# Weight loads of the dense pairs one pair sooner, high key/query stores issued by ScalarE, in a two-layer hybrid decoder trunk

## The chip, the cores and the metric

The kernel runs on 1 core of one Trainium2 chip. The metric is the device time of one launch in microseconds (us). Engines are named as in the profile: PE is TensorE, DVE is VectorE, ACT is ScalarE, POOL is GpSimd, SP is SyncE. SP has no arithmetic here: it issues DMAs. A DMA-issuing instruction is listed with a q after its engine (SPq).

## The reference, cut to what matters

All data are float32: x is 1 x 1024 x 1024, there are two layers, and each layer does

```python
h = rmsnorm(x, norm1[l])
proj = h @ w_in[l]                      # q, k, v of both mixers, and the gates
o_a = dilated_mixture(...)              # 12 heads of 64 in 3 groups: (window, dilation) = (128,1), (512,4), (2048,16)
o_b = stick_breaking_attention(...)     # 4 heads of 64
gates = sigmoid(gate_pre + b_gate[l]); g_a, g_b = gates[..., :1024], gates[..., 1024:]
x = x + (g_a * (o_a @ w_br[l, :256]) + g_b * (o_b @ w_br[l, 256:])) @ w_o[l]
h2 = rmsnorm(x, norm2[l])
a, v = split(h2 @ w_up[l])              # each 2816 wide
x = x + (gelu(causal_depthwise_conv(a)) * v) @ w_down[l]
```

and a last rmsnorm follows. The change touches only how the part `h @ w_in[l]` for the dilated groups 1 and 2 and for the gates is fed.

## The kernel before

**Split products.** Every float32 matrix product is done as three reduced-precision ones. An operand is split in two: ACT writes the high part (a cast, line 129), DVE subtracts it from the operand and writes the low part (line 130); `split` is that pair of instructions. PE then adds high x high, high x low and low x high.

**The mixer's items.** In each layer the attention work is a list of items: 16 stick-breaking items (named B), 4 near items (N, dilation 1) and 16 far items (T, the dilated groups 1 and 2). A far item makes scores z (line 584), DVE adds the bias and finds the row's extreme (line 795), ACT takes the exponential (796), PE transposes (803 to 805), `split` makes p1h and p1l, and PE applies them to the values (line 813). `attend` lets PE go on with a quantum of dense work (`Dense.advance`) after each piece of an item.

**The dense work.** The projections for groups 1 and 2 and for the gates come as fourteen pairs a layer: v1, k/q 1 of heads 0 and 1, k/q 2 of the same, v2, then k/q 1 and k/q 2 of heads 2 and 3, and eight gate pairs. A pair is a 2 x 2 block of products: 256 columns of weights by the two halves of the tokens. One block (token half 1, first columns) is done early and plainly by `ahead`; the first half of its sum is kept in DRAM as q1. The rest of a pair is done by `pair_rest` with fewer products: sums of weight blocks (on POOL and DVE: lines 990, 991, 993 and 998) meet sums of blocks of h (made once a layer by `block_sums`, tiles S[1] to S[4]). `seven` is one such product: 12 matmuls of 128 x 512 (lines 887 to 889). A pair needs five of them, with weight pieces called w6, w5, w7, w3 and w4 in that order of use; `piece` takes a slot for the high and the low part (four slots of each) and splits.

**Buffers around the change.** The raw weights of a pair are one tile `in_a` of four 128 x 512 blocks (a11, a12, a21, a22), with two slots (tag "ql"). Before the change the result r2 is written over a12, and the stores of r2 read it from there, so the slot stays taken until those are done. The tile `u` holds two blocks: u2 = a11 - a21 (made into w7) and u1, the q1 read back.

**The order.** PE follows the program's order. On ACT, DVE, POOL and SP a scheduler arranges the instructions of the mixer by when it expects them to be ready. Each engine then runs its list strictly in order. `Dense.ready` calls the first steps of a pair (up to `READY` = 6) while the pair before is being computed: the load of `in_a` is the first of these steps, so it stands in the program after the start of the pair before.

**Stores of keys and queries.** `put` in `pair_kq` writes a block's high part (tile kq_h) and low part, and stores both to DRAM (tk) as 64 x 4 x 128 pieces: 4 stores for a key block, 6 for a query block, 20 for a k/q pair (4 of them in `ahead`), all from SP. Far items read them back as t_kq (line 755), and values as t_v (line 761).

**Semaphores of DMAs.** DMAs that SP and ACT issue share eight completion semaphores by turns, and the program lets a DMA wait until the DMA eight before it in that count is complete.

Of the kernel before, what the change touches and what calls it, by code (L numbers as in the profile page):

```python
# [6 lines left out]
F32 = mybir.dt.float32  # L7
# [8 lines left out]
P = 128  # L16
# [36 lines left out]
def trunk_kernel(ctx, tc, x, norm1, w_in, b_gate, w_br, w_o, norm2, w_up, conv_w, conv_b, w_down, norm_f, out, depth=None, probe=None):  # L53
# [141 lines left out]
    class Dense:  # L195
# [2 lines left out]


        def __init__(self):  # L200
            self.main, self.plain, self.seven, self.done = [], [], [], set()
            self.side, self.later, self.hooks = [], {}, []
            self.now = self.nxt = None
            self.due, self.count = 0.0, 0
            self.started = False
            self.scored = self.applied = self.kq = self.v = 0
# [686 lines left out]
    def block_sums():  # L893


        keep = {}

        def first(t, a, b, i):
            if i == 0:
                if "r" not in keep:  # L900
                    keep["r"] = quarter("h_sum")
                new_s(t)
            r, (ah, al), (bh, bl) = keep["r"][:, i, :], a()[i], b()[i]
            pool.tensor_tensor(r, f32(al), f32(bl), ALU.subtract)
            pool.tensor_tensor(r, r, f32(ah), ALU.add)
            pool.tensor_tensor(r, r, f32(bh), ALU.subtract)

        def further(t, a, i):
            if t == 4:

                S[4] = half(0, 0)
            elif i == 0:
                new_s(t)
            r, (ah, al) = keep["r"][:, i, :], a()[i]
            dve.tensor_tensor(r, f32(ah), r, ALU.subtract)
            dve.tensor_tensor(r, r, f32(al), ALU.add)

        def in_two(t, i):
            split(*S[t][i], keep["r"][:, i, :])

        b11, b12, b21, b22 = (lambda n=n, k=k: half(n, k) for k in range(2) for n in (1, 0))
        todo = []

        def series(after, t, f, lag, gap):

            at = {}
            for i in range(4):
                at.setdefault(i * gap, []).append(lambda i=i: f(i))
                at.setdefault(i * gap + lag, []).append(lambda i=i: in_two(t, i))
            for k in range(3 * gap + lag + 1):  # L930
                todo.append((after, lambda fs=at.get(k, ()): [g() for g in fs]))

        series({"B17"}, 3, lambda i: first(3, b22, b12, i), 4, 3)
        series({"N01s"}, 1, lambda i: first(1, b12, b11, i), 4, 3)
        series({"N11s"}, 2, lambda i: further(2, b22, i), 1, 1)
        series({"plain", "01", "v0"}, 4, lambda i: further(4, b21, i), 1, 1)
        return todo
# [10 lines left out]
    def pair(dense, l, offs, tiled, put):  # L948

        key = offs[0]  # L950

        def view(x, n=None):

            return x.rearrange("p (r j) -> p r j", r=4) if tiled else x

        def grid(o):
            return o.rearrange("p (j r) -> p r j", r=4) if tiled else o

        def ahead():

            w = weights(w_in[l][:, offs[0] : offs[0] + P], P)
            yield
            t, f = small("q1s"), small("rf")
            o = bank("ps", "r_ps")
            yield from product(o, [(w[k], h_part(1, k)) for k in range(4)])
            act.copy(view(t), grid(o))
            nc.sync.dma_start(kept_product(key), t)
            yield
            o = bank("ps", "r_ps")
            yield from product(o, [(w[k], h_part(1, k)) for k in range(4, KD)])  # L970
            dve.tensor_tensor(view(f), view(t), grid(o), ALU.add)
            put(0, 1, f, False)
            yield

        return ahead, lambda: pair_rest(dense, l, offs, put, view, grid, kept_product(key))

    def pair_rest(dense, l, offs, put, view, grid, kept):

        raw = sb.tile([P, 4, 512], F32, tag="ql", bufs=2, name="in_a")
        for c in range(2):  # L980
            nc.sync.dma_start(
                raw[:, 2 * c : 2 * c + 2, :].rearrange("p a (k n) -> p (a k) n", n=P),
                w_in[l][:, offs[c] : offs[c] + P].rearrange("(k p) n -> p k n", p=P),
            )
        a11, a12, a21, a22 = (raw[:, i, :] for i in range(4))
        yield
        u = sb.tile([P, T], F32, tag="wr", bufs=NRAW, name="u")
        u1, u2 = u[:, HF:T], u[:, 0:HF]
        nc.sync.dma_start(u1, kept)
        pool.tensor_tensor(u2, a11, a21, ALU.subtract)  # L990
        pool.tensor_tensor(a21, a21, a22, ALU.add)  # L991
        yield
        dve.tensor_tensor(a11, a21, a11, ALU.subtract)
        w5 = piece(a21)
        yield
        w6 = piece(a11)
        yield
        pool.tensor_tensor(a11, a12, a11, ALU.subtract)
        yield
        w3 = piece(a11)  # L1000
        yield
        u5 = small("u5")
        pa, pc = bank("ps", "i_a"), bank("ps", "i_c")
        yield from seven(pa, w6, S[2], True, True)
        r2 = a12
        dve.tensor_tensor(view(r2), view(u1), grid(pa), ALU.add)
        w7 = piece(u2)
        yield "turn"
        yield
        yield from seven(pc, w5, S[1], True, True)  # L1010
        dve.tensor_tensor(view(u5), view(u1), grid(pc), ALU.add)
        w4 = piece(a22)
        dense.last(0)
        yield "turn"
        yield
        yield from seven(pa, w7, S[3], False, True)
        dve.tensor_tensor(view(u5), view(u5), grid(pa), ALU.add)
        put(1, 0, u5, False)
        yield "turn"
        yield  # L1020
        yield from seven(pc, w3, half(0, 1), False, True)
        dve.tensor_tensor(view(r2), view(r2), grid(pc), ALU.add)
        put(0, 0, r2, False)
        dense.last(1)
        yield "turn"
        yield
        for word in seven(pa, w4, S[4], False, True):
            yield "turn"
            yield
        dve.tensor_tensor(view(u1), view(u1), grid(pa), ALU.add)  # L1030
        put(1, 1, u1, False)
        yield

    def pair_kq(dense, l, g, pr):
        off = 256 * g + P * pr

        def put(c, n, x, psum):
            hi = small("kq_h", F32R)
            lo = small("kq_l", F32R) if psum else x.bitcast(F32R)
            hv, lv, xv = (t if t is x and psum else t.rearrange("p (r j) -> p r j", r=4) for t in (hi, lo, x))  # L1040
            if c:
                act.mul(hv, xv, -SCALE)
                dve.scalar_tensor_tensor(lv, xv, -SCALE, f32(hv), ALU.mult, ALU.subtract)
            else:
                act.copy(hv, xv)
                dve.tensor_tensor(lv, xv, f32(hv), ALU.subtract)
            for s in range(2):
                rows = slice(64 * s, 64 * s + 64)
                for src, kind, up in ((hv, c, 0), (hv, 1, 64), (lv, 2, 0)) if c else ((hv, 0, 0), (lv, 0, 64)):
                    there = tk[pr][s, :, up : up + 64, 3 * (g - 1) + kind, n * P : (n + 1) * P]  # L1050
                    nc.sync.dma_start(there.rearrange("r p j -> p r j"), f32(src[rows]))
            if (c, n) == (1, 1):
                dense.done.add(f"{g}{pr}")

        return pair(dense, l, (OFF_KA + off, OFF_QA + off), True, put)
# [63 lines left out]
    def mixer(l, pending):  # L1119
# [13 lines left out]
        dense.plain = [a() for a, _ in [*kqs.values(), *vs.values(), *gates]]  # L1133
        dense.seven = [rest() for _, rest in gates]
        dense.side = [({"B02"}, zeros)] * (l == 0) + block_sums()

        def kq(name, pr, after, off, scale):
# [707 lines left out]
```

## Time and profile before

| what | value |
|---|---|
| median of 3 runs | 2802.39 us (2801.98 to 2808.36) |
| the profiled execution | 2802.19 us, its span 2800.4 us |
| mean granted TensorE clock | 0.985 |
| layer 0: dense pairs beside near and far items, then gate pairs | about 330 to 615 us |
| layer 1: the same | about 1715 to 2005 us |

The profiled execution's own time is 0.2 us below the median, and 1.8 us of it lie outside the span. A page of the profile lists busy time by engine, the costliest groups of instructions with the idle time before them and what ended it, and the DMA issues; the trace behind it answers for any window. In a timeline row the columns are the start, the duration, engine, line, operation, tiles and count, and in brackets the idle time of the engine just before with what ended it. In a row of waits stand who waited for whom, the total, the number of times and the longest.

### The profile page before, as it was taken

The page shows a single profiled execution, that of the slowest core. Times are in us where ns is not written, and L with a number is a line of the kernel's source. Part 1 is how long each engine was busy: PE and PEld are TensorE (multiplying, and loading weights), DVE is VectorE, ACT ScalarE, POOL GpSimd, SP SyncE. Part 2 cuts the span into 40 slices and gives each one's busy share as a digit, 9 for nine tenths or more (in the row PEclk, how much of TensorE's full clock was granted, in tenths as well). Part 3 has the DMA queues.
Part 4 walks back from the last instruction along what each step waited for, and adds up shares of the span by engine and source line. Part 5 has one row for each costly group of instructions (what it writes and reads, how often), then busy time and mean ns, then how long its engine had stood idle before and what let it go on. Part 6 is the DMA issues. An engine that isn't in the chain of part 4 may idle for free. (4 is left out here: it accounts for less than half of the span.)

```text
span 2800.4 us, 37074 instructions
## 1 busy us (share of the span) xinstructions
PE 2689.2 (96%) x13098; PEld 2244.5 (80%) x13098; DVE 2087.0 (75%) x3132; ACT 1327.8 (47%) x2458; POOL 692.2 (25%) x509
## 2 busy tenths in 40 slices
PE   8998989989999999999999899889899999999999
PEld 8877868778888888878888778677788888888888
DVE  5886856656688888897657877565667899888965
ACT  5665524346455455532345655333454555554225
POOL 1004121213224343421210041121131334433210
PEclk9999999999999999999999999999999999999999
DMA  5033378545324444588411234775643344446873
GB/s 152 23 87 102 114 212 245 197 158 190 104 91 157 154 141 158 195 327 315 163 35 46 82 101 134 222 229 177 225 129 90 113 166 153 145 154 233 323 262 121
DMA packets 394629, 449.91 MB, mean 161 GB/s; under 512 B 22748, under 2 KB 315980, under 8 KB 392908
## 3 DMA queue, kind: packets, MB, share of 16 engines
q1 hardware_dynamic: 394444, 447.55, 48.5%
q8 instruction: 103, 1.69, 0.3%
q14 instruction: 82, 0.67, 0.1%
HBM read 300.61 MB, written 146.87 MB: 160 GB/s over the span
## 5 line engine op out<-in xcount | busy, mean ns | idle before, releaser
L130 DVE TENSOR_TENSOR w_lo<-up_a,w_hi 128x512 fp32r<-128x512 f32 x240 | 236.7, 993 | 20.2 <-ACT w_hi L129 20.2
L129 ACT CAST w_hi<-up_a 128x512 fp32r<-128x512 f32 x240 | 149.4, 622 | 184.1 <-PE u_a L888 45.8
L1601 DVE TENSOR_TENSOR x<-x,d_ps 128x512 f32<-128x512 f32 (+1 forms) x228 | 151.9, 671 | 77.0 <-PE d_ps L1595 75.6
L1332 POOL TENSOR_TENSOR cv<-cv 128x512 f32<-128x512 f32 x88 | 131.8, 1509 | 249.3 <-DVE cv L1327 139.4
L129 ACT CAST w_hi<-w_raw 128x512 fp32r<-128x512 f32 x176 | 109.2, 621 | 147.8 <-PE o_ps L156 68.3
L130 DVE TENSOR_TENSOR w_lo<-w_raw,w_hi 128x512 fp32r<-128x512 f32 x176 | 127.5, 728 | 69.5 <-ACT w_hi L129 68.7
L130 DVE TENSOR_TENSOR g<-cv,g 128x512 fp32r<-128x512 f32 x154 | 152.2, 989 | 5.2 <-ACT g L129 2.8
L1593 PE MATMUL d_ps<-gd_in,w_hi 128*128 128x512 f32 (+1 forms) x340 | 130.3, 383 | 2.3 <-ACT w_hi L129 1.1
L129 ACT CAST w_hi<-in_a 128x512 fp32r<-128x512 f32 x112 | 69.2, 619 | 131.6 <-POOL in_a L991 43.5
L990 POOL TENSOR_TENSOR u<-in_a 128x512 f32<-128x512 f32 x28 | 38.4, 1373 | 374.4 <-DMA in_a<-in_w_in_dram 211.9
L1595 PE MATMUL d_ps<-gd_in,w_lo 128*128 128x512 f32 (+1 forms) x340 | 129.8, 382 | 0.0
L1594 PE MATMUL d_ps<-gd_in,w_hi 128*128 128x512 f32 (+1 forms) x340 | 129.7, 382 | 0.0
L887 PE MATMUL u_a<-hh,w_hi 128*128 128x512 f32 x320 | 124.7, 390 | 0.5 <-DVE u L1483 0.5
L889 PE MATMUL u_a<-hh,w_lo 128*128 128x512 f32 x320 | 124.5, 389 | 0.0
L889 PE MATMUL u_a<-t_hi,w_lo 128*128 128x512 f32 x320 | 124.5, 389 | 0.0
L888 PE MATMUL u_a<-t_lo,w_hi 128*128 128x512 f32 x320 | 124.5, 389 | 0.0
L888 PE MATMUL u_a<-hl,w_hi 128*128 128x512 f32 x320 | 124.5, 389 | 0.0
L887 PE MATMUL u_a<-t_hi,w_hi 128*128 128x512 f32 x320 | 124.5, 389 | 0.0
L1593 PE MATMUL d_ps<-gd_in,wd 128*128 128x512 f32 (+1 forms) x292 | 113.9, 390 | 0.0
L1595 PE MATMUL d_ps<-gd_in,wd 128*128 128x512 f32 (+1 forms) x292 | 112.8, 386 | 0.0
L1594 PE MATMUL d_ps<-gd_in,wd 128*128 128x512 f32 (+1 forms) x292 | 112.8, 386 | 0.0
L129 ACT CAST g<-cv 128x512 fp32r<-128x512 f32 x154 | 94.9, 616 | 36.9 <-POOL cv L1332 29.4
(392 smaller groups left out, 8734.3 us busy)
## 6 DMA issues: line engine op xcount, KB each, us to landing
gd<-g SPq DMA_DIRECT2D x154, 512.0 KB, 3.6
gd_in<-gd SPq DMA_DIRECT2D x154, 512.0 KB, 6.6
up_a<-in_w_up_dram SPq DMA_DIRECT2D x80, 512.0 KB, 5.8
in_a<-in_w_in_dram SPq DMA_DIRECT2D x56, 512.0 KB, 5.5
w_raw<-in_w_in_dram SPq DMA_DIRECT2D x104, 256.0 KB, 3.0
t_kq<-tk SPq DMA_DIRECT2D x32, 768.0 KB, 5.4
wd_raw<-in_w_down_dram SPq DMA_DIRECT2D x22, 1024.0 KB, 8.4
gin<-gs SPq DMA_DIRECT2D x32, 512.0 KB, 4.4
```

What stands on the lines that cost most here:

```text
L129: act.copy(hi, src)
L130: dve.tensor_tensor(lo, src, f32(hi), ALU.subtract)
L887: pe.matmul(o, w[0][:, c], rh, start=(first and i == 0), stop=False, skip_group_check=True)
L888: pe.matmul(o, w[0][:, c], rl, start=False, stop=False, skip_group_check=True)
L889: pe.matmul(o, w[1][:, c], rh, start=False, stop=(last and i == 3), skip_group_check=True)
L990: pool.tensor_tensor(u2, a11, a21, ALU.subtract)
L1332: return lambda: pool.tensor_tensor(dst, a, b, ALU.subtract)
L1593: pe.matmul(o[:, sub], wh[:, c], gh[:, sub], start=(i == 0 and k in (0, 4, 5)), stop=False, skip_group_check=True)
L1594: pe.matmul(o[:, sub], wh[:, c], gl[:, sub], start=False, stop=False, skip_group_check=True)
L1595: pe.matmul(o[:, sub], wl[:, c], gh[:, sub], start=False, stop=(i == m - 1), skip_group_check=True)
L1601: dve.tensor_tensor(x, x, o[:, sub], ALU.add)
```

## The change

1. `pair_rest` gives back two things: the generator `run` and a function `load` that takes the `in_a` slot and issues the load. The loads of a layer are queued in `dense.loads` in the order of the pairs. When a pair has split its last piece w4, the next load in the queue is issued: that of the pair after the next. The first two pairs of a layer call their load at their own start, as all did before.
2. r2 is written into u2 instead of a12, so an `in_a` slot comes free when w4 is split.
3. The pieces are split in their order of use: w6, w5, w7 before the first product, w3 after it, w4 after the second. The two sums on POOL at the start are separate steps.
4. In `pair_kq`, stores whose source is the high part (12 of 20 a pair) are issued by ACT. Those of the low part stay on SP.
5. In `block_sums` the lag from a sum to its split goes from 4 steps to 6, and the gap from sum to sum from 3 to 4, for S[3] and S[1].

```diff
@@ block_sums
-        series({"B17"}, 3, lambda i: first(3, b22, b12, i), 4, 3)
-        series({"N01s"}, 1, lambda i: first(1, b12, b11, i), 4, 3)
+        series({"B17"}, 3, lambda i: first(3, b22, b12, i), 6, 4)
+        series({"N01s"}, 1, lambda i: first(1, b12, b11, i), 6, 4)
@@ pair_rest: the load becomes a function
+        raw = []
+        def load():
+            raw.append(sb.tile([P, 4, 512], F32, tag="ql", bufs=2, name="in_a"))
+            for c in range(2):
+                nc.sync.dma_start(
...
+        def run():
+            if not raw:
+                assert dense.loads.pop(0) is load
+                load()
...
-        dve.tensor_tensor(a11, a21, a11, ALU.subtract)
-        w5 = piece(a21)
-        yield
-        w6 = piece(a11)
-        yield
-        pool.tensor_tensor(a11, a12, a11, ALU.subtract)
-        yield
-        w3 = piece(a11)
-        yield
+            dve.tensor_tensor(a11, a21, a11, ALU.subtract)
+            w6 = piece(a11)
+            yield
+            pool.tensor_tensor(a11, a12, a11, ALU.subtract)
+            w5 = piece(a21)
+            yield
+            w7 = piece(u2)
+            yield
...
-        r2 = a12
+            r2 = u2
             dve.tensor_tensor(view(r2), view(u1), grid(pa), ALU.add)
-        w7 = piece(u2)
+            w3 = piece(a11)
...
             w4 = piece(a22)
+            if dense.loads:
+                dense.loads.pop(0)()
             dense.last(0)
@@ pair_kq, put
-                    nc.sync.dma_start(there.rearrange("r p j -> p r j"), f32(src[rows]))
+                    (nc.sync if src is lv else act).dma_start(there.rearrange("r p j -> p r j"), f32(src[rows]))
@@ mixer
+        order = [vs[1], *(kqs[g, 0] for g in (1, 2)), vs[2], *(kqs[g, 1] for g in (1, 2)), *gates]
+        dense.loads = [load for _, _, load in order]
```

What moves, in the lists of instructions of the engines. PE's list stays as it was, row for row. The list of SP in layer 0, before, around the load of the fourth pair, v2 (in_a_3839); tk0 and tk1 hold the stored keys and queries, tv the values, the numbers count buffers, and kq_h_3779 to u_3557 are blocks of the second pair:

```order
L1051 DMA tk0_90<-kq_h_3779 64x4x128 x2
L1051 DMA tk0_90<-u5_3705 64x4x128
L1051 DMA tk0_90<-kq_h_3805 64x4x128
L1051 DMA tk0_90<-in_a_3526 64x4x128
L1051 DMA tk0_90<-kq_h_3805 64x4x128
L1051 DMA tk0_90<-in_a_3526 64x4x128
L1051 DMA tk0_90<-kq_h_3830 64x4x128 x2
L1051 DMA tk0_90<-u_3557 64x4x128
L1051 DMA tk0_90<-kq_h_3830 64x4x128 x2
L1051 DMA tk0_90<-u_3557 64x4x128
L981 DMA in_a_3839<-in_w_in_dram 128x8x128 x2
L989 DMA u_3862<-q1_726 128x512
```

The same place on SP after the change (in_a_3760 is the fourth pair's load, in_a_3882 the fifth's; u_3740 belongs to the third pair, u_3862 to the fourth):

```order
L996 DMA u_3740<-q1_718 128x512
L1082 DMA tv1_93<-vv_3719 128x2x128 x2
L1082 DMA tv1_93<-vv_3724 128x2x128 x2
L983 DMA in_a_3760<-in_w_in_dram 128x8x128 x2
L1062 DMA tk0_90<-u5_3705 64x4x128 x2
L1062 DMA tk0_90<-u_3557 64x4x128 x4
L996 DMA u_3862<-q1_716 128x512
L983 DMA in_a_3882<-in_w_in_dram 128x8x128 x2
```

Before, a pair's load stands directly ahead of its own u and behind the second pair's stores; now the fourth pair's load stands ahead of those stores, and the fifth's directly behind the fourth pair's u: each a pair sooner. Of the sixteen stores that `pair_rest` makes for a k/q pair, six are left on SP.

ACT's list in layer 0 before, at the first far items (p1 rows are exponentials, p1h rows the high parts that PE waits for):

```order
L1042 ACTIVATE kq_h_4174<-u5_4091 128x512
L129 COPY w_hi_4214<-in_a_4088 128x512
L1045 COPY kq_h_4200<-in_a_3961 128x512
L796 ACTIVATE p1_4222,st1_4218<-p1_4222,st1_4218 128x256
L796 ACTIVATE p1_4222,st1_4218<-p1_4222,st1_4218 128x512
L129 COPY w_hi_4307<-u_4135 128x512
L1042 ACTIVATE kq_h_4244<-u_3984 128x512
L129 COPY p1h_4274<-t1_4270 128x384
L796 ACTIVATE p1_4255,st1_4218<-p1_4255,st1_4218 128x256
L796 ACTIVATE p1_4255,st1_4218<-p1_4255,st1_4218 128x512
```

The same place on ACT after:

```order
L1053 ACTIVATE kq_h_4172<-u5_4091 128x512
L1062 DMA tk1_91<-kq_h_4172 64x4x128 x4
L1056 COPY kq_h_4199<-u_3984 128x512
L129 COPY w_hi_4217<-u_4135 128x512
L1062 DMA tk1_91<-kq_h_4199 64x4x128 x2
L796 ACTIVATE p1_4225,st1_4221<-p1_4225,st1_4221 128x256
L796 ACTIVATE p1_4225,st1_4221<-p1_4225,st1_4221 128x512
L1053 ACTIVATE kq_h_4247<-u_3984 128x512
L129 COPY p1h_4277<-t1_4273 128x384
L1062 DMA tk1_91<-kq_h_4247 64x4x128 x2
L129 COPY p1h_4296<-t1_4292 128x384
L1062 DMA tk1_91<-kq_h_4247 64x4x128 x2
```

Ten DMA issues (six, two and two) now stand between ACT's own work and the exponentials and p1h casts behind them. Over both layers ACT's list gains 96 DMA issues, and SP's loses as many.

At the sums of h the wider spacing moves nothing: POOL's list there is the same before and after, and so are the places of the splits t_hi on ACT, in both layers. Before and after, the first of S[1]'s sums follow those of S[3] on POOL as

```order
L905 TENSOR_TENSOR h_sum<-h_sum,hh_108 128x512 x2
L906 TENSOR_TENSOR h_sum<-h_sum,hh_108 128x512 x2
L904 TENSOR_TENSOR h_sum<-hl_109,hl_363 128x512
L905 TENSOR_TENSOR h_sum<-h_sum,hh_108 128x512
L904 TENSOR_TENSOR h_sum<-hl_109,hl_363 128x512
L906 TENSOR_TENSOR h_sum<-h_sum,hh_362 128x512
L905 TENSOR_TENSOR h_sum<-h_sum,hh_108 128x512
```

which shows that the scheduler placed them by readiness, whatever the steps between them in the program.

More of the change, by code (lines that the diff above doesn't have):

```diff
@@ L200, in __init__ @@
         def __init__(self):
-            self.main, self.plain, self.seven, self.done = [], [], [], set()
+            self.main, self.plain, self.seven, self.loads, self.done = [], [], [], [], set()
             self.side, self.later, self.hooks = [], {}, []
@@ L973, in ahead @@
             yield
-        return ahead, lambda: pair_rest(dense, l, offs, put, view, grid, kept_product(key))
+        return (ahead, *pair_rest(dense, l, offs, put, view, grid, kept_product(key)))
     def pair_rest(dense, l, offs, put, view, grid, kept):
[L979 to L984, printed above, removed]
@@ L985, in pair_rest @@
-        a11, a12, a21, a22 = (raw[:, i, :] for i in range(4))
-        yield
[L987 to L991, printed above, removed]
-        yield
-        dve.tensor_tensor(a11, a21, a11, ALU.subtract)
-        w5 = piece(a21)
-        yield
-        w6 = piece(a11)
-        yield
-        pool.tensor_tensor(a11, a12, a11, ALU.subtract)
@@ L999, in pair_rest @@
-        yield
-        w3 = piece(a11)
[L1001 to L1004, printed above, removed]
-        r2 = a12
-        dve.tensor_tensor(view(r2), view(u1), grid(pa), ALU.add)
-        w7 = piece(u2)
[L1008 to L1027, printed above, removed]
+        raw = []
[3 more added lines that the diff above has]
+                nc.sync.dma_start(
+                    raw[0][:, 2 * c : 2 * c + 2, :].rearrange("p a (k n) -> p (a k) n", n=P),
+                    w_in[l][:, offs[c] : offs[c] + P].rearrange("(k p) n -> p k n", p=P),
+                )
@@ new lines, in run @@
+        def run():
+            if not raw:
+                assert dense.loads.pop(0) is load
+                load()
+            a11, a12, a21, a22 = (raw[0][:, i, :] for i in range(4))
+            yield
+            u = sb.tile([P, T], F32, tag="wr", bufs=NRAW, name="u")
+            u1, u2 = u[:, HF:T], u[:, 0:HF]
+            nc.sync.dma_start(u1, kept)
+            pool.tensor_tensor(u2, a11, a21, ALU.subtract)
+            yield
+            pool.tensor_tensor(a21, a21, a22, ALU.add)
+            yield
+            dve.tensor_tensor(a11, a21, a11, ALU.subtract)
+            w6 = piece(a11)
+            yield
+            pool.tensor_tensor(a11, a12, a11, ALU.subtract)
+            w5 = piece(a21)
+            yield
+            w7 = piece(u2)
+            yield
+            u5 = small("u5")
+            pa, pc = bank("ps", "i_a"), bank("ps", "i_c")
+            yield from seven(pa, w6, S[2], True, True)
+            r2 = u2
+            dve.tensor_tensor(view(r2), view(u1), grid(pa), ALU.add)
+            w3 = piece(a11)
@@ L1028, in pair_rest @@
             yield "turn"
             yield
-        dve.tensor_tensor(view(u1), view(u1), grid(pa), ALU.add)
-        put(1, 1, u1, False)
-        yield
+            yield from seven(pc, w5, S[1], True, True)
+            dve.tensor_tensor(view(u5), view(u1), grid(pc), ALU.add)
+            w4 = piece(a22)
+            if dense.loads:
+                dense.loads.pop(0)()
+            dense.last(0)
+            yield "turn"
+            yield
+            yield from seven(pa, w7, S[3], False, True)
@@ new lines, in run @@
+            dve.tensor_tensor(view(u5), view(u5), grid(pa), ALU.add)
+            put(1, 0, u5, False)
+            yield "turn"
+            yield
+            yield from seven(pc, w3, half(0, 1), False, True)
+            dve.tensor_tensor(view(r2), view(r2), grid(pc), ALU.add)
+            put(0, 0, r2, False)
+            dense.last(1)
+            yield "turn"
+            yield
+            for word in seven(pa, w4, S[4], False, True):
+                yield "turn"
+                yield
@@ L1034, in pair_kq @@
+            dve.tensor_tensor(view(u1), view(u1), grid(pa), ALU.add)
+            put(1, 1, u1, False)
+            yield
+        return run, load
     def pair_kq(dense, l, g, pr):
@@ L1132, in mixer @@
         gates = [pair_gate(dense, l, e) for e in range(KD)]
-        dense.plain = [a() for a, _ in [*kqs.values(), *vs.values(), *gates]]
-        dense.seven = [rest() for _, rest in gates]
+        dense.plain = [a() for a, _, _ in [*kqs.values(), *vs.values(), *gates]]
+        dense.seven = [rest() for _, rest, _ in gates]
+        order = [vs[1], *(kqs[g, 0] for g in (1, 2)), vs[2], *(kqs[g, 1] for g in (1, 2)), *gates]
+        dense.loads = [load for _, _, load in order]
         dense.side = [({"B02"}, zeros)] * (l == 0) + block_sums()
```

## The prediction

> **What bounds the kernel now.** I read the page first, then busy time by stage, then PE's waits in the two stages that hold the dense pairs, then the timelines of single stalls. From the page:
>
> ```profile
> span 2800.4 us, 37074 instructions
> PE 2689.2 (96%) x13098; PEld 2244.5 (80%) x13098; DVE 2087.0 (75%) x3132; ACT 1327.8 (47%) x2458; POOL 692.2 (25%) x509
> L990 POOL TENSOR_TENSOR u<-in_a 128x512 f32<-128x512 f32 x28 | 38.4, 1373 | 374.4 <-DMA in_a<-in_w_in_dram 211.9
> in_a<-in_w_in_dram SPq DMA_DIRECT2D x56, 512.0 KB, 5.5
> ```
>
> PE sets the time, and the change leaves PE's list as it is: it can win only idle time of PE and time at a reduced clock. POOL's first step on a pair's weights (L990) waits 211.9 us for the load. By stage (PE, PEld, DVE, ACT, POOL busy; then the granted clock):
>
> ```profile
> 330.00:615.00 285.00, 258.77 (x1306) 214.32 (x1305) 177.29 (x337) 109.46 (x227) 58.56 (x48) 0.96 0.62 192
> 850.00:900.00 50.00, 50.00 (x222) 41.42 (x221) 44.48 (x47) 26.76 (x43) 23.19 (x15) 1.00 0.40 137
> 1715.00:2005.00 290.00, 260.88 (x1316) 216.33 (x1315) 180.64 (x342) 111.29 (x230) 58.64 (x48) 0.96 0.63 195
> ```
>
> In the FFN (850 to 900) PE is busy throughout at full clock. In the two stages of pairs it idles 26.2 and 29.1 us, and a clock of 0.96 loses another 0.04 x 285 = 11.4 and 0.04 x 290 = 11.6 us. PE's longest waits in these stages, layer 0 first:
>
> ```profile
> PE o L813 <- DVE p1l L130: 11.3, 6, 4.3
> PE i_a L887 <- ACT w_hi L129: 7.1, 2, 5.4
> PE z L584 <- DVE st L795: 4.0, 2, 3.3
> ...
> PE o L813 <- DVE p1l L130: 13.5, 6, 3.9
> PE i_a L887 <- ACT w_hi L129: 7.7, 2, 6.0
> PE z L584 <- DVE st L795: 4.3, 2, 3.6
> ```
>
> Only the second of each three names a weight piece. The timelines show that the others too come from late weights. First the plain case, the fourth pair of layer 0 (SP, POOL, PE):
>
> ```profile
> 375.16 1.29 SPq L1051 DMA_DIRECT2D tk<-kq_h  x2
> 376.49 0.62 SPq L1051 DMA_DIRECT2D tk<-u  x1
> 377.22 1.26 SPq L981 DMA_DIRECT2D in_a<-in_w_in_dram  x2
> 383.70 1.26 POOL L990 TENSOR_TENSOR u<-in_a 128x512 f32<-128x512 f32 x1 [16.43 <-DMA in_a<-in_w_in_dram]
> 387.87 0.79 PE L887 MATMUL i_a<-t_hi,w_hi 128*128 128x512 f32 x1 [5.42 <-ACT w_hi L129]
> ```
>
> SP issues the load only at 377.22, behind the stores; POOL starts at 383.70, PE at 387.87, 5.42 us late. Now a far item (POOL, DVE, PE):
>
> ```profile
> 492.39 1.29 POOL L990 TENSOR_TENSOR u<-in_a 128x512 f32<-128x512 f32 x1 [10.26 <-DMA in_a<-in_w_in_dram]
> 493.76 1.27 POOL L991 TENSOR_TENSOR in_a<-in_a 128x512 f32<-128x512 f32 x1
> 495.06 0.69 DVE L993 TENSOR_TENSOR in_a<-in_a 128x512 f32<-128x512 f32 x1 [3.46 <-POOL in_a L991]
> 495.67 0.55 DVE L130 TENSOR_TENSOR p1l<-t,p1h 128x384 fp32r<-128x384 f32 x1
> 496.27 0.39 PE L813 MATMUL o<-p1l,t_v 128*128 128x256 f32 x1 [1.98 <-DVE p1l L130]
> ```
>
> DVE runs in order. Its L993 waits 3.46 us for POOL, which waited for the load; the p1l split that PE needs is queued behind L993. So one late load delays attention that has nothing to do with it.
>
> The clock follows the stalls:
>
> ```profile
> 388.00:391.40 3.40, 3.40 (x8) 2.39 (x9) 1.36 (x3) 1.14 (x2) 1.27 (x1) 0.50 0.80 192
> 496.50:500.00 3.50, 3.50 (x16) 2.98 (x16) 3.15 (x9) 1.07 (x2) 1.35 (x3) 0.63 0.20 15
> 1956.30:1960.00 3.70, 3.63 (x21) 3.20 (x22) 3.43 (x7) 1.10 (x2) 0.00 (x0) 1.00 0.00 0
> 1956.37 0.39 PE L813 MATMUL o<-p1l,t_v 128*128 128x256 f32 x1 [2.24 <-DVE p1l L130]
> ```
>
> After the 5.42 us gap PE has half clock, after the 1.98 us gap 0.63 over 3.5 us, after a gap of 2.24 us nothing: a stall of about 2 us may cost as much again. [...]
>
> **The change part by part.**
>
> Loads sooner, r2 out of `in_a`, split order. The load moves one pair ahead. POOL idled 16.43 us ahead of 383.70, and PE was late by 5.42; a pair's five products of 12 matmuls take PE 60 x 0.39 = 23 us (half of the 0.79 that the row at half clock shows), so a load one pair sooner has far more room than any of these stalls asks for. With r2 in u2 the slot depends on a split by DVE, not on stores. Splitting in the order of use frees each of the four piece slots earlier and costs nothing: the same five splits. So I count the waits on late weights as gone. Two of the p1l waits have another cause (a split behind a w_lo) and stay:
>
> ```profile
> 522.65 0.38 PE L813 MATMUL o<-p1l,t_v 128*128 128x256 f32 x1 [0.30 <-DVE p1l L130]
> 599.36 0.38 PE L813 MATMUL o<-p1l,t_v 128*128 128x256 f32 x1 [1.13 <-DVE p1l L130]
> ```
>
> Layer 0 then wins 11.3 - 1.4 = 9.9 (p1l), 7.1 (w_hi) and of z's 4.0 a chosen 2.3 (the shorter wait of 0.7 and 1.0 of the longer left standing): 19.3. Layer 1 the same way 13.5 - 1.4 + 7.7 + 2.6 = 22.4. With the clock's 11.4 and 11.6, since every stall that halved it is one of these, **64.7 us**.
>
> Stores on ACT. The trace has no DMA issued by ACT; its nearest rows are SP's issues of the same stores, and ACT's idle time ahead of the work that PE waits for:
>
> ```profile
> L1051 SPq DMA_DIRECT2D tk<-kq_h x96: 574/611/2105, 147.9 to 1833.3; - x96
> ACT p1h L129 <- PE t L805: 25.4, 14, 3.7
> ACT p L796 <- DVE st L795: 20.0, 17, 3.0
> ACT beta L624 <- DVE z L623: 15.8, 12, 2.2
> 350.00:400.00 50.00, 43.68 (x188) 34.78 (x187) 26.34 (x41) 12.93 (x23) 10.24 (x8) 0.93 0.72 195
> ```
>
> At 0.61 us an issue, ACT waits for its own input 25.4 / 14 = 1.8 us before a p1h, 20.0 / 17 = 1.2 before an exponential, 15.8 / 12 = 1.3 before a beta. Among far items ACT's list has six issues ahead of one exponential (3.7 us, 2.5 beyond the cover), four ahead of another (2.4 us, 1.2 beyond), and single groups of two (1.2 us, covered): 3.7 us a layer. One stall of that size can cost a piece of clock, 1.7 us. So 5.4 a layer, 10.8 in all; the low end is 0, the high end every one of the 2 x 20 issues there at 0.61, 24 us. Where the first two k/q pairs run, ACT is busy 12.93 of 50 us, and I take nothing. The four groups of two a layer that `ahead` makes among the stick-breaking items have 1.2 us against a cover of 1.3: 0 to 4.9 us a layer, I take 1, so 2 in all.
>
> A store also waits for the DMA eight before it in the common count. Where that is a load that lands after 5.5 us, with seven issues of 0.61 between, 5.5 - 4.3 = 1.2 us of ACT are at stake; I take 1 us a layer, bounds 0 and three such a layer, 3.6 (7.2 in all). Cost of ACT's issues: 10.8 + 2 + 2 = **14.8 us**. [...]
>
> SP keeps 96 issues less, and what follows there (reads of t_kq, t_v, u) comes sooner or as before: nothing taken.
>
> Sums spaced wider. POOL, DVE and ACT have the same order there before and after, so these stalls stay (PE's waits between 255 and 295, then the window's clock in both layers):
>
> ```profile
> PE o L713 <- ACT p0h L129: 3.2, 1, 3.2
> PE o L713 <- DVE p0l L130: 1.9, 2, 1.3
> PE r_ps L155 <- ACT q1s L966: 1.1, 1, 1.1
> ...
> 265.00:290.00 25.00, 21.51 (x90) 17.35 (x91) 21.69 (x39) 16.87 (x36) 13.42 (x10) 0.80 0.37 107
> 1650.50:1675.50 25.00, 21.29 (x89) 17.16 (x90) 21.75 (x39) 17.13 (x38) 13.71 (x10) 0.80 0.38 111
> 260.35 0.62 ACT L129 CAST t_hi<-h_sum 128x512 fp32r<-128x512 f32 x1 [5.78 <-POOL h_sum L906]
> ```
>
> They are worth 3.2 + 1.9 + 1.1 + 0.20 x 25 = 11.2 us a layer: ACT's t_hi waits 5.78 us for POOL's sum with the p0h cast behind it. Taken: 0; bound 22.4 us gained.
>
> Sum: 2802.2 - 64.7 + 14.8 = 2752.3; the median is 0.2 above the profiled execution: **2752 us**.
>
> **The rivals.**
>
> *More is won.* The sums' waits go too (2752 - 22 = 2730), or ACT's issues are hidden (2738), or both (2715). For it: ACT is busy only 109 of 285 us in the stage. Against it: the same order at the sums. I count it at 2730 or so; chance 0.15.
>
> *The next thing is late.* With the load gone, DVE still does L993, five splits and the far items in one line, and a p1l may meet another wait, as at 599.36. If only half of the waits on p1l and z goes (half of 9.9 + 12.1 + 2.3 + 2.6, that is 13.5) with the w_hi waits (14.8) and half of the clock (11.5), the gain is 39.8 - 14.8 = 25: 2777 us. Against it: the rows show DVE idle for 3.46 us ahead of L993, not busy. Chance 0.20.
>
> *Slower: ACT's issues cost more than SP's.* The 96 issues fall into groups of two and four. With some 1.5 us of cover for each of about 32 groups the loss is 96 x X - 48 us for an issue of X us; it equals 64.7 at X = 1.17, about twice SP's median, and ACT holds casts and exponentials behind them, so PE, DVE and all follow. At X = 1.4 the loss is 86 and the time 2824 us. For it: single issues of 2.1 us on SP (2105 ns). Against it: the median of 0.61, and groups with far more cover where the first pairs run. Chance 0.10.
>
> *It does not do what it says.* The load is issued sooner but waits as long, since SP itself waits on a common semaphore ahead of it: 2800 us, chance 0.05.
>
> **How the numbers follow.** The forecast has 0.50, with a range of its own from 2738 (ACT free) to 2778 (ACT's costs at their high ends, 24.4 + 9.8 + 7.2 = 41.4 instead of 14.8). To 0.8 belong also the larger gain down to 2722 and the next-late case up to 2790; below is left the case of both at 2715, above slower and no change. A measurement of this kernel can tell about 0.3%, 8.4 us, from no change. Faster by more: 0.50 + 0.15 + 0.20 = 0.85; within it 0.05; slower 0.10.
>
> **What would show it.** Right: POOL's L990 (now another line) waits no longer for the load in either stage of pairs; w_hi leaves PE's waits on i_a, the p1l waits fall to about 1.4 us a layer plus ACT's new ones; the clock of both stages rises from 0.96 to 0.99; ACT's issues take 0.6 us; the sums' stalls around 265 and 1651 stand as they were. Wrong: p1h or exponentials late behind ACT's stores with PE idle over 10 us a layer, issues on ACT of over 1.2 us, or the clock still at 0.96.

## The result, and the profile after

| | before | after |
|---|---|---|
| median, 4 runs each | 2805.23 us | 2775.90 us (2772.82 to 2779.93) |
| profiled execution, span | 2800.4 us | 2778.1 us |
| ratio after to before | | 0.9896, 95% interval 0.9876 to 0.9917 |

The kernel became 1.0% faster: some 29 us where 50 were forecast. The profiled execution after is the slowest of its four, so the two spans differ by 22.3 us only. The page after:

```profile
span 2778.1 us, 37044 instructions
PE 2688.1 (97%) x13098; PEld 2241.6 (81%) x13098; DVE 2091.8 (75%) x3132; ACT 1327.2 (48%) x2458; POOL 695.2 (25%) x509
```

Its two stages of pairs, by windows (nearly the same matmuls as 330 to 615 and 1715 to 2005 before; the length, then PE, PEld, DVE, ACT and POOL busy, the granted clock, the DMA share and GB/s):

```profile
332.60:606.10 273.50, 255.75 (x1303) 210.58 (x1302) 179.40 (x338) 108.87 (x227) 57.66 (x47) 0.98 0.66 202
1708.10:1983.10 275.00, 257.65 (x1313) 212.20 (x1312) 181.80 (x341) 110.17 (x230) 58.18 (x48) 0.98 0.67 205
```

From the same matmul to the same matmul the stages are 10.8 and 14.2 us shorter. PE idles 17.8 and 17.4 us in them instead of 26.2 and 29.1, and the clock is at 0.98 instead of 0.96. The rest of the trace took back some 3 us: PE comes to the first stage 2.9 us later than before. What PE waits for there now, layer 0:

```profile
PE t L803 <- ACT p L796: 3.2, 2, 2.2
PE v_t L1074 <- DVE u L1026: 3.0, 1, 3.0
PE o L813 <- DVE p1l L130: 2.3, 5, 1.1
PE o L813 <- ACT p1h L129: 2.2, 2, 1.6
PE z L584 <- DVE st L795: 2.0, 2, 1.8
```

The p1l waits fell from 11.3 to 2.3 us, z from 4.0 to 2.0, and i_a's wait for w_hi from 7.1 to 0.9; in layer 1 they fell from 13.5 to 2.4, 4.3 to 2.3 and 7.7 to 1.6. Two waits are new, on exponentials and ahead of v_t (2.0 and 2.1 us in layer 1). What POOL waits for at its first step on a pair (whole span):

```profile
POOL u L997 <- DMA gs<-u: 80.5, 7, 13.2
POOL u L997 <- DMA tk<-kq_h: 69.1, 5, 17.9
POOL u L997 <- DMA tk<-u: 17.9, 1, 17.9
```

The load, 211.9 us before, is gone from here. Stores are in its place, most of them of an earlier pair out of u: the load came sooner, but the slot of u did not. (Stores of kq_h neither read nor write u. Where a row names one, another DMA on a shared semaphore may have held POOL; the trace does not settle it.) At the first far-item place that the prediction showed, POOL still starts at the very time of before (492.39 there), now right behind the last store of u, yet DVE's line loses far less:

```profile
487.14 3.45 SPq L1102 DMA_DIRECT2D gs<-u  x2
492.38 1.28 POOL L997 TENSOR_TENSOR u<-in_a 128x512 f32<-128x512 f32 x1 [10.85 <-DMA gs<-u]
495.07 0.69 DVE L1001 TENSOR_TENSOR in_a<-in_a 128x512 f32<-128x512 f32 x1 [1.16 <-POOL in_a L999]
498.10 0.56 DVE L130 TENSOR_TENSOR p1l<-t,p1h 128x384 fp32r<-128x384 f32 x1
```

PE comes to the product just ahead, that of p1h, 4.8 us later than before (498.77 against 494.01), so the same time on the clock is sooner in its work; DVE waits 1.16 us for POOL instead of 3.46, and PE not at all. The stall that is new at v_t (ACT, DVE, POOL, DVE, DVE, PE):

```profile
390.40 4.41 ACTq L1062 DMA_DIRECT2D tk<-kq_h  x4
395.50 0.69 DVE L130 TENSOR_TENSOR w_lo<-in_a,w_hi 128x512 fp32r<-128x512 f32 x1 [1.50 <-ACT w_hi L129]
396.38 1.28 POOL L997 TENSOR_TENSOR u<-in_a 128x512 f32<-128x512 f32 x1 [10.08 <-DVE w_lo L130]
399.03 0.69 DVE L1001 TENSOR_TENSOR in_a<-in_a 128x512 f32<-128x512 f32 x1 [2.83 <-POOL in_a L999]
399.64 0.68 DVE L1026 TENSOR_TENSOR u<-u,i_a 128x512 f32<-128x512 f32 x1
400.38 0.66 PE L1074 MATMUL v_t<-ident,u 128*128 128x128 f32 x4 [3.02 <-DVE u L1026]
```

It is the old pattern: DVE waits for POOL with something behind it that PE needs, here a sum for the transposes of v. POOL's start is put down to a w_lo of DVE, which waited for a cast on ACT behind four stores (the first two rows).

### The profile page after: what moved, and what is told of

It is laid out like the page before. It is cut to its first block, busy times and chain, and to the rows that moved or that the text cites. A ratio compares the mean times of both kernels' runs of the same rounds, so it can differ in the third digit from the quotient of the medians.

```text
span 2778.1 us, 37044 instructions
## 1 busy us (share of the span) xinstructions
PE 2688.1 (97%) x13098; PEld 2241.6 (81%) x13098; DVE 2091.8 (75%) x3132; ACT 1327.2 (48%) x2458; POOL 695.2 (25%) x509
```

## The experiments

Each run is timed against the kernel before on the same chip. To compare kernels across chips, use the ratios to before.

| run | what | median us | ratio to before (95%) |
|---|---|---|---|
| after | the whole change | 2775.9 | 0.9896 (0.9876 to 0.9917) |
| e1 | after, stores on SP | 2770.2 | 0.9880 (0.9862 to 0.9899) |
| e2 | before, stores on ACT | 2821.9 | 1.0066 (1.0047 to 1.0084) |
| e3 | after, r2 in a12 | 2810.1 | 1.0024 (1.0013 to 1.0035) |
| e4 | after, old spacing | 2776.8 | 0.9902 (0.9884 to 0.9920) |
| e5 | after, late results in in_a | 2839.9 | 1.0124 (1.0110 to 1.0138) |
| e6 | after, old split order | 2771.8 | 0.9880 (0.9867 to 0.9894) |
| e7 | before, r2 in u2 | 2765.8 | 0.9859 (0.9845 to 0.9872) |
| e8 | after, sums split on POOL | 2805.3 | 1.0001 (0.9992 to 1.0010) |
| e9 | e7, lag 12 | 2760.2 | 0.9838 (0.9824 to 0.9853) |
| e10 | e7, stores on ACT | 2772.8 | 0.9885 (0.9867 to 0.9903) |
| e11 | e7, loads sooner | 2759.4 | 0.9837 (0.9822 to 0.9852) |
| e12 | e11, lag 12 | 2757.4 | 0.9827 (0.9813 to 0.9842) |

**e1: stores on SP again.**

```diff
-  (nc.sync if src is lv else act).dma_start(there...
+  nc.sync.dma_start(there...
```

> The changed kernel with all stores of keys and queries on SP again; loads a pair sooner, r2 in u2 and the split order stay. Theory (the gain comes from the sooner loads, and the stores on ACT only delay exponentials and casts behind them): the stalls of PE on exponentials at about 431 and 452 (0.97, 2.23 us) and 1828 (1.99 us) with a clock piece each go, some 5 us a layer: about 2766 us, 2762 to 2772. Rival (the stores had to leave SP, since sixteen of them at 0.6 us still stand ahead of the reads of t_kq, t_v and q1): PE waits on z or on weight pieces by several us a pair, 2785 us or more.

2770.2 us; by ratio 0.16% below the whole change, with overlapping intervals, so the time alone does not show a gain. The rival falls, and the theory's stalls on exponentials are gone, and with them the one at v_t, but a z stall of 4.1 us stood in their place. In the trace after, the stall at 452 comes about so (ACT, ACT, PE):

```profile
447.52 3.97 ACTq L1062 DMA_DIRECT2D tk<-kq_h  x4
451.55 0.51 ACT L796 ACTIVATE p<-p,st 128x256 f32<-128x256 f32 x1 [3.54 <-issue]
452.20 0.33 PE L803 MATMUL t<-ident,p 128*128 128x128 f32 x1 [2.23 <-ACT p L796]
```

Four stores hold ACT for 4 us; the exponential is behind them, and PE waits 2.23 us.

**e2: only the stores on ACT.** The same line, changed in the kernel before.

> The kernel before with one edit: high parts of keys and queries are stored by ACT. Theory (sooner loads are what counts): the train of stores ahead of a load shrinks from 10 us to 4, so the two weight stalls at 388 and 406 shrink, but the stalls of the far items beside gate pairs (496, 565, 588) stay, and ACT's stalls of some 5 us a layer are added: 2795 us, 2787 to 2803. Rival (the train of stores on SP is the cause, and moving it off is the gain): within 6 us of the changed kernel, 2776 to 2782.

2821.9 us, slower than before. Both theory and rival are missed; the rival is far off. The stores on ACT alone cost 0.7%, and the load is no sooner for it: POOL waits 233.2 us for loads in this run, 211.9 before. Why the loss of some 18 us is larger than what the stores on ACT cost in the other runs (4 to 12 us) was not followed further.

**e3: r2 over a12 again, loads still a pair sooner.**

```diff
-            r2 = u2
+            r2 = a12
```

> The changed kernel with r2 written over a12 of in_a again, so that the next load waits for r2's stores or gate output to leave the slot, about two products (9 us) later than a split of w4. Theory (a pair sooner leaves so much room that the slot's release no longer matters, and the u slot, held by u's last stores, is what POOL waits for now): the same within 4 us, 2772 to 2780, and u released no later. Rival (r2 in u2 is needed for the gain): POOL waits for the load again and the stalls of the far items return in part: 2785 us or more.

2810.1 us: the whole gain gone, and the far items' stalls are back (12.0 us on p1l in layer 0). The theory falls in its time, the rival in its wait. What POOL waits for:

```profile
POOL u L997 <- DMA gs<-u: 139.5, 10, 15.8
POOL u L997 <- DMA tk<-u: 111.8, 6, 21.5
POOL u L997 <- DMA in_a<-in_w_in_dram: 5.2, 2, 2.9
```

Not for the load, but for stores out of u, 251 us against 98 in the whole change. Its SP and POOL in gate pairs:

```profile
493.62 0.38 SPq L1102 DMA_DIRECT2D gs<-in_a  x1
496.82 1.01 SPq L983 DMA_DIRECT2D in_a<-in_w_in_dram  x2
497.92 1.05 SPq L1102 DMA_DIRECT2D gs<-u  x1
503.28 1.28 POOL L997 TENSOR_TENSOR u<-in_a 128x512 f32<-128x512 f32 x1 [12.80 <-DMA gs<-u]
```

Though the program issues the load a pair sooner, it stands on SP behind r2's store and starts 3.2 us after it. The last store of u follows right behind the load, and POOL starts 5.4 us after that store's issue. Before, SP had nearly the same order (the load's second half stood behind u's store), and the load started at the same distance from r2's store:

```profile
482.38 0.38 SPq L1091 DMA_DIRECT2D gs<-in_a  x1
485.60 0.38 SPq L981 DMA_DIRECT2D in_a<-in_w_in_dram  x1
486.07 0.53 SPq L1091 DMA_DIRECT2D gs<-u  x1
486.66 0.43 SPq L981 DMA_DIRECT2D in_a<-in_w_in_dram  x1
```

So here it is the slot of in_a, and not the line of the program, that sets when a load starts, and a load that has to wait holds up the store of u behind it on SP. The sooner load alone was not run: e3 has the stores on ACT and the new split order too. Against e2, which has the stores alone, e3 is 0.4% faster (the intervals do not meet), so the sooner loads may win something there.

**e4: the old spacing.**

```diff
-        series({"B17"}, 3, lambda i: first(3, b22, b12, i), 6, 4)
-        series({"N01s"}, 1, lambda i: first(1, b12, b11, i), 6, 4)
+        series({"B17"}, 3, lambda i: first(3, b22, b12, i), 4, 3)
+        series({"N01s"}, 1, lambda i: first(1, b12, b11, i), 4, 3)
```

> The changed kernel with the sums' lag and gap at 4 and 3 again. The lists differ only in where the later sums (S[2], S[4]) and their splits stand, some steps sooner. Theory (spacing does nothing for the stalls at the first sums): stalls at 265 and 1651 unchanged, time the same within 3 us, 2773 to 2779. Rival (spacing is worth something behind the sums, at the start of the pairs around 344 to 364): 2780 us or more.

2776.8 us: no difference, as the theory had it. The places of the first sums and their splits are the same; only the later sums, S[2] and S[4], stand a few rows elsewhere.

**e5: both late results in in_a, the load at the pair's end.**

```diff
-            r2 = u2
+            r2 = a12
...
-            if dense.loads:
-                dense.loads.pop(0)()
             dense.last(0)
...
-            dve.tensor_tensor(view(u1), view(u1), grid(pa), ALU.add)
-            put(1, 1, u1, False)
+            dve.tensor_tensor(view(a11), view(u1), grid(pa), ALU.add)
+            put(1, 1, a11, False)
+            if dense.loads:
+                dense.loads.pop(0)()
```

> The changed kernel with both late results (r2, and the last block that was u1) written into in_a, and the next load issued at the pair's end instead of after w4: u is now free as soon as DVE has read it, in_a only when the last stores are done. Theory (POOL's start on a pair waits for the u slot, which the last stores from u hold): POOL waits no longer for stores of u, the stalls at 400 and 1776 (3.0 and 2.1 us before v_t, with their clock) go: about 2766 us, 2760 to 2772. Rival (SP, which runs in order, now stands at the load until the last stores have landed, and delays what is behind it, as with r2 in a12): 2785 us or more.

2839.9 us: the rival. POOL does not wait for stores of u any more, but longer for the load than in the kernel before:

```profile
POOL u L997 <- DMA in_a<-in_w_in_dram: 267.5, 18, 20.0
```

Freeing u at in_a's expense is the wrong way round: a load of two times 512 KB has to follow the release of in_a, while u needs only POOL's first step and a reading back of 256 KB.

**e6: the pieces split in the old order.** w5, w6 and w3 at the start, w7 after the first product.

> The changed kernel with the pieces split in the order of the kernel before (w5, w6, w3 at the start, w7 after the first product, w4 after the second). Theory (the order is not what limits): 2771 to 2781 us. Rival (a piece that is split when its turn is near holds PE, 12 pairs or so by 0.5 to 1 us a layer): 2785 us or more.

2771.8 us, 0.16% below the whole change, with overlapping intervals: as the theory had it, if anything faster.

**e7: r2 in u2, alone, in the kernel before.**

```diff
+        w7 = piece(u2)
-        r2 = a12
+        r2 = u2
         dve.tensor_tensor(view(r2), view(u1), grid(pa), ALU.add)
-        w7 = piece(u2)
```

> The kernel before with one edit: r2 is written into u2 (w7 split just ahead of it); loads stand where they stood, stores on SP. Theory (SP stood at a load that waited for in_a's slot, with the last store from u, which holds the u slot, queued behind it; r2 in u2 ends that wait): the far items' stalls beside gate pairs shrink and about half of the gain comes from this edit alone: 2785 us, 2776 to 2793. Rival (only the place of the load counts): 2798 us or more.

2765.8 us: 39 us from one edit, more than the whole change has (the intervals of the ratios do not meet). More than the theory expected, and the rival falls. The load's code is where it was, yet SP now issues the fourth pair's load ahead of the second pair's stores, at 360.94 us instead of 377.22; only the place of r2 is another:

```profile
356.04 0.44 SPq L989 DMA_DIRECT2D u<-q  x1
356.78 3.80 SPq L1071 DMA_DIRECT2D tv<-vv  x4
360.94 1.00 SPq L981 DMA_DIRECT2D in_a<-in_w_in_dram  x2
364.83 1.24 SPq L1051 DMA_DIRECT2D tk<-kq_h  x2
```

And in a gate pair (SP, SP, POOL, DVE):

```profile
476.10 0.45 SPq L981 DMA_DIRECT2D in_a<-in_w_in_dram  x1
482.21 0.32 SPq L1091 DMA_DIRECT2D gs<-u  x1
484.33 1.29 POOL L990 TENSOR_TENSOR u<-in_a 128x512 f32<-128x512 f32 x1 [7.13 <-DMA gs<-u]
487.03 0.69 DVE L993 TENSOR_TENSOR in_a<-in_a 128x512 f32<-128x512 f32 x1 [1.18 <-POOL in_a L991]
```

The last store of u is no longer issued right behind a load: POOL starts 2.1 us after its issue, against 5.4 in e3. DVE waits 1.18 us for POOL.

**e8: the first sums split by POOL.**

```diff
-            split(*S[t][i], keep["r"][:, i, :])
+            hi, lo = S[t][i]
+            if t in (1, 3):
+                pool.tensor_copy(hi, keep["r"][:, i, :])
+                pool.tensor_tensor(lo, keep["r"][:, i, :], f32(hi), ALU.subtract)
+            else:
+                split(hi, lo, keep["r"][:, i, :])
```

> The changed kernel with S[3] and S[1] split by POOL (a copy and a subtraction, 16 more operations of 1.3 to 1.7 us a layer), so that no cast on ACT waits for POOL's sums. Theory (a cast on ACT that waits 5.8 us for POOL holds the p0h that PE needs): the stalls of 3.2, 1.3, 0.6 and 1.1 us at 268 to 289 and their halved clock go, 11 us a layer: 2754 us, 2750 to 2762. Rival (another wait takes their place, such as the first pair's sums coming 24 us later): 2768 us or more.

2805.3 us: the rival. ACT's cast no longer waits, but the next sums (DVE, L915) wait for POOL's last splits, with p0l behind them:

```profile
287.91 5.89 DVE L915 TENSOR_TENSOR h_sum<-hh,h_sum 128x512 f32<-128x512 f32 x2 [19.64 <-POOL t_lo L922]
296.08 0.47 PE L713 MATMUL o<-p0l,v 128*128 128x128 f32 x1 [22.10 <-DVE p0l L130]
```

**e9: e7 with lag 12 and gap 3 in both series.**

> The kernel before with r2 in u2, and the sums of h spaced so that it moves them: lag 12, gap 3 puts the first split t_hi of S[3] some 20 places later in ACT's list, behind the p0h casts; at 6 and 4 it had not moved. Theory (a split of the sums placed ahead of p0h on ACT is what stalls PE at 265 to 285): these stalls and their halved clock go, 11 us a layer, so against r2 alone (2766 us) 2744, 2740 to 2752. Rival (POOL's sums take as long, and something else waits for them, as when POOL made the splits): 2762 us or more.

2760.2 us, 0.2% below e7 with overlapping intervals: between the two expectations. The wider spacing now moves the splits, and the stall moves with them (PE, 255 to 300):

```profile
PE o L713 <- DVE p0l L130: 5.1, 2, 3.6
PE o L713 <- ACT p0h L129: 1.8, 1, 1.8
```

Against e7 p0h fell from 3.2 to 1.8 us, but p0l rose from 1.9 to 5.1: DVE's half of the split is queued like ACT's. PE waits there longer, not shorter; what is better is the granted clock, 0.992 over the profiled execution instead of 0.988.

**e10: e7 with the high parts stored by ACT.**

> The kernel before with r2 in u2 and the high parts stored by ACT. Theory (issues on ACT delay exponentials and casts there, and SP's shorter train no longer matters once the load can pass it): 5 to 15 us above r2 alone: 2770 to 2781. Rival (SP's train still holds loads back, as at 441 where a load issued at 427 landed at 435 and z waited 4.8 us): 2762 us or less.

2772.8 us, 7 us above e7, as the theory had it (the intervals just overlap): exponentials hold PE for 3.1 us in layer 0, as after.

**e11: e7 with the sooner loads, nothing else.**

> The kernel before with r2 in u2 and the loads issued a pair sooner in the program; stores on SP, pieces split in the old order, old spacing. Theory (once the slot is free the scheduler has already moved the load: SP's list has it within a few rows of the same place): the same as r2 alone, 2762 to 2771 us. Rival (the program's place still counts): 2758 us or less.

2759.4 us, 0.22% below e7 by ratio, the intervals just overlapping: between theory and rival. SP's lists are alike to within a few rows up to the sixth pair, as the theory had it; the load of the first gate pair is ahead of the reads of t_kq instead of between them, and the z stall there is 0.96 us instead of 4.76. So the sooner loads seem worth a little, some 6 us, once r2 is out.

**e12: e11 with lag 12.**

> The kernel before with r2 in u2, loads a pair sooner, and the sums' lag 12 and gap 3. Theory (the two do not touch each other): the gain of lag 12 again, as much below r2 with the sooner loads as the other run with lag 12 lies below r2 alone: about 2744, 2738 to 2752. Rival (later splits delay the first pairs): 2762 us or more.

2757.4 us: between theory and rival. The lag's gain on top of e11 is 0.1%, well inside the intervals, so it is not shown. It is the lowest time of all, 1.7% below before, and 0.7% below the whole change with intervals apart; from e9 and e11 it cannot be told. The granted clock is 1.00 in both stages of pairs.

## Why the prediction was right, and where its steps were not

The direction and the place were right: PE's waits on p1l, z and w_hi in the two stages fell, and with them the clock's loss. The path was as shown: a late load, POOL, DVE in order, a split that PE needs. That the time fell into the forecast's own range was in part luck. The gain was counted about twice too large and the cost of the stores too large as well, and the two errors partly cancel. The range reached up to 2778 us for dear stores on ACT, not for a small gain, and 2775.9 is no nearer to the forecast than to the rival that the next thing is late (2777).

**Loads sooner, r2, split order, counted together at 64.7 us.** This is the step that failed, in size and in what it credited. Measured without the stores on ACT (e1) the three are worth 33.7 us (2803.84 to 2770.17). In the trace after, the waits that were counted fell nearly as counted, by 36 of 42 us (p1l, w_hi and z, both layers), but PE's idle time in the two stages fell by 20 us only: other waits came, and of these the sum had only those behind the stores on ACT. And the prediction led with the place of the load in the program. e3 shows that without r2 in u2 the sooner load does not bring the gain, e7 that r2 alone wins 39 us, and e11 that the sooner loads add some 6 to that. It had noted that r2 made the slot depend on DVE instead of stores, but not that this dependence was what placed the load.

Where the gain lies can be read from the traces, since PE's list is the same in all these kernels: set a matmul of one trace beside the same matmul of the other. The windows are those of the trace before. Below is the time that PE gains (-) or loses (+) against before, one execution each, in us. The first part of a stage runs until the last keys and queries are stored, the second is gate pairs and far items.

| run | r2 in | stores | 330 to 460 | 460 to 615 | 1715 to 1845 | 1845 to 2005 |
|---|---|---|---|---|---|---|
| after | u2 | ACT | +2.2 | -13.0 | +1.2 | -15.4 |
| e10 | u2 | ACT | +1.5 | -13.1 | -5.2 | -16.1 |
| e1 | u2 | SP | -5.5 | -10.9 | -4.6 | -12.0 |
| e7 | u2 | SP | -3.2 | -13.9 | -3.8 | -16.9 |
| e11 | u2 | SP | -8.7 | -12.3 | -9.3 | -15.1 |
| e3 | a12 | ACT | +9.8 | -4.3 | +6.2 | -6.1 |
| e2 | a12 | ACT | +11.9 | -7.7 | +11.7 | -0.6 |

With r2 in u2 the second parts win 11 to 17 us whatever else is changed. The whole change wins nothing in the first parts, where the weights came late most plainly (5.42 us): what the w_hi waits gave there, other waits took back.

**The split order, taken as free,** costs some 11 us where SP makes the stores: e11 and e1 differ in it and in the spacing, which e4 showed to be worth nothing in the changed kernel. The ratio rises from 0.9837 to 0.9880, the intervals not meeting. With the stores on ACT (e6) the cost is 4 us and not clear of the noise. "The same five splits" was true, but their place was not free. In e1 (DVE, then PE) the split of w7 out of u now stands with two others ahead of a far item's L795:

```profile
435.22 1.30 DVE L130 TENSOR_TENSOR w_lo<-in_a,w_hi 128x512 fp32r<-128x512 f32 x2
436.43 1.75 DVE L130 TENSOR_TENSOR w_lo<-u,w_hi 128x512 fp32r<-128x512 f32 x1
438.11 0.67 DVE L1039 TENSOR_TENSOR u<-u,i_a 128x512 f32<-128x512 f32 x1
438.70 0.41 DVE L795 CUSTOM_DVE_ANT_1 p<-z,bias 128x256 f32<-128x256 f32 x1
439.18 0.44 PE L584 MATMUL z<-t_kq 128*128 128x128 f32 x1 [4.09 <-DVE st L795]
```

In e11, with two splits there, the wait is 0.96 us (PE):

```profile
439.95 0.33 PE L584 MATMUL z<-t_kq 128*128 128x128 f32 x1 [0.96 <-DVE st L795]
```

The split of w7 is not all of that difference of 3.1 us. From DVE's sum on in_a behind POOL to its L795 it takes 4.86 us in e1 (from 433.84) and 3.06 in e11 (from 436.41), so 1.8 us are the split's; for the rest POOL had started less far ahead of PE. In e7, with the old split order, this wait is 4.76 us. What makes up the 11 us was not followed through.

**A next late thing,** a rival with 0.20, came in part: in POOL's waits the u slot, which r2 now holds too, took the load's place. The prediction named p1l for it and did not look at u's slot. The 3.0 us at v_t are not the slot's work alone: with r2 in u2 this wait stands in every run that stores from ACT (2.9 to 3.2 us in layer 0 in after, e4, e6 and e10, 2.1 in e8), and in none that stores from SP (e1, e7, e9, e11, e12). So it belongs to the price of the stores on ACT.

**Stores on ACT, 14.8 us.** One issue on ACT takes what SP's took (median 0.636 us against 0.611):

```profile
L1062 ACTq DMA_DIRECT2D tk<-kq_h x96: 582/636/1712, 149.7 to 1825.3; - x96
```

The cost is 4 us by e1 and 7 by e10 (in both the intervals overlap), 12 by e6 against e11 (which differ also in the spacing), and 18 by e2, where r2 was still in in_a. With r2 out it is below the term, in e2 above it, and always within its bounds. It came at the place that was named, exponentials behind four stores (2.23 us against the 1.2 beyond cover that were worked out, since the four took 4.0 us and not 2.4: 0.58, 0.66, 1.06 and 1.56), and at one that was not, the casts of weights ahead of v_t. The rival of issues twice as dear as SP's did not come. No kernel with the stores on ACT was faster than its like with the stores on SP (by ratio to before 0.9896 after against 0.9880 in e1, 0.9885 in e10 against 0.9859 in e7, and 1.0066 in e2), so here what SP saved in issues was worth no more than ACT's own time.

**Sums spaced wider, 0 us:** right (e4). The stalls of 3.2 and 1.1 us are still there after; e8 and e9 show that moving the work passes the wait on to DVE.

**The clock** was to rise to 0.99 in both stages and rose to 0.98: it stands at 0.50 for 10.2 us of each stage instead of 23.9, in layer 0 for 3.41 us each from 401.65, 452.85 and 524.53, behind the new stalls at 400, 452 and 522.

## What to carry to other kernels

When a scheduler orders the DMAs, ask what a transfer waits for before asking where it is issued: a load can move no further ahead than the release of its buffer, and a result parked in an input buffer delays the next input until it is stored. Split a change of several edits early: here one line was worth more than the whole, and two of its companions, the stores on ACT and the split order, won nothing or cost time. On an engine that runs in order, ask of every instruction that moves what stands behind it and who waits for that, even if the number of instructions stays the same.

## What the runs showed of the hardware

The same gap of PE was charged in one run and not in another. In the trace before, a gap of 2.19 us among the stick-breaking items is followed by full clock, in the trace after the same gap by 3.4 us at 0.57. Before (PE's row, then the window behind it):

```profile
184.18 0.33 PE L638 MATMUL sb_t<-ident,beta 128*128 128x128 f32 x1 [2.19 <-DVE beta L628]
184.20:187.60 3.40, 3.40 (x19) 2.93 (x19) 3.35 (x7) 2.40 (x6) 0.00 (x0) 1.00 0.27 77
```

And after:

```profile
186.04 0.33 PE L638 MATMUL sb_t<-ident,beta 128*128 128x128 f32 x1 [2.19 <-DVE beta L628]
186.10:189.50 3.40, 3.40 (x13) 2.85 (x14) 3.21 (x7) 1.79 (x5) 0.00 (x0) 0.57 0.27 77
```

So the length of a gap alone did not tell whether the clock fell behind it. The gap of 2.24 us that the prediction found uncharged, ahead of 1956.37, is followed by a clock of 1.00 up to 1978.8; the one of 1.98 us ahead of 496.27 is followed by 0.50 from 497.43 to 500.84. What else decides it is left open here.

POOL's start on a pair came 5.4 us after the issue of u's last store where a load of two times 512 KB went out just before (e3), and 2.1 us after it where none did (e7). These are single places; no run varied this alone.
